# Seven-product up projection: all products of a half unit made wide, the third factor summed by an adding transfer, and another order of the seven

## The chip, the cores and the metric

One core of one Trainium2 chip runs the whole kernel. The metric is the device time of one execution in microseconds (us), given as the median of several runs. The profile beside it is one execution taken by the hardware profiler. A difference of 0.3% is 5.7 us here.

## The reference, cut to what matters

One layer on a sequence of 512 tokens and 2048 channels, in float32: a mixing part (attention and pooling), then a gated feed-forward part. The change touches only the up projection of the second part:

```python
h = rms_norm(x, pre_ffn_g[l])
up = causal_dwconv(h @ w_up[l], conv_w[l], conv_b[l])          # w_up: 2048 x 11264
y = (gelu(up[..., :D_FF], approximate=True) * up[..., D_FF:]) @ w_down[l]
x = x + rms_norm(y, post_ffn_g[l])
```

## The kernel before

**Precision.** Every float32 operand is kept as two parts, a high part rounded to fp32r and the remainder. Making them from a weight block of 128 x 1024 takes two steps of `split`: ACT writes the high part (`wfh`, L143, "rounding" below), DVE subtracts it from the block and writes the low part (`wfl`, L144, "remainder"). A product then needs high x high, high x low and low x high.

**Half units.** The up projection is cut into 44 half units `k` (0 to 43), each of 256 output channels. Half unit `k` is a 2 x 2 block product done with seven block products instead of eight. `i` from 1 to 7 names a product and the weight factor that goes with it; `seven(k, i)` (L941) issues it. Odd half units close a unit: there the gate of the even half is multiplied with the convolved odd half.

**Two forms of a product.** The plain form (L948, `mm3` L159 to L161) has 24 matmuls of 256 columns, three for each of eight weight blocks. The wide form (`wide`, L954 to L962) has eight matmuls of 512 columns, in which the high weights meet the high and the low half of `h` side by side, and eight of 256 columns for the low weights. Its two halves of 256 columns in the bank must be added afterwards. From half unit 5 on (`EARLY = 5`, `PAIRED = 4`) products 3 to 7 are wide; 1 and 2 are plain, and share bank 0, a half each.

**Emptying the banks.** Bank 0: `begin_z` (L880), an ACT copy and one DVE add, after product 2. Bank 1 (product 6): `finish_six` (L892), two DVE adds out of the bank and then two in SBUF. Products 5 and 7: one pair of banks, `keep_pair` (L886). Products 3 and 4: two pairs in turn, by `k % 2`, emptied by two DVE adds of `keep_all` (L1194); then the convolution runs (`taps`: ACT L1155, DVE L1156 and L1157, two of each), in odd half units two DVE products (L1173) and the store of the gate from POOL's queue.

**Weight factors.** A factor is a sum of weight blocks, formed in place: a block is loaded by a DMA from SP's queue (L623), and further blocks are added by DMAs with `accum_op=add` from POOL's queue (L803), each issued once the factor made before from the same buffer has its remainder. Buffer `x` serves factors 4, 5, 6 and 3 in turn, `y` serves 1 and 7, `z` serves 2 and, in half units 5 and later, is added to `x` by DVE (L811) for factor 3.

**Order.** The tensor engine runs in the order of the program; ACT, DVE and POOL run in order too, in an order that a planner fixes when the kernel is built: of the instructions that are ready it takes the one that stands first in the program. `Factors` makes each factor four products ahead, and there are four pairs of `wfh`/`wfl`: the factor of product n+4 goes into the pair that product n leaves. The order of the seven products is written out in `self.order`. In a half unit `k` it is 4, 1, 2, then 6 and 3 of `k - 1`, then 5 and 7. After product 1 of each half unit from 6 on, one of 32 steps that sum `w_down` blocks for the next stage is issued (`wd_sums`), half as copies from SP's queue, half as adding transfers from POOL's.

Of the kernel before, what the change touches and what calls it, by code (L numbers as in the profile page):

```python
# [11 lines left out]
AF = mybir.ActivationFunctionType  # L12
# [18 lines left out]
EARLY = 5  # L31
PAIRED = EARLY - 1
CU = 4
AHEAD = 3
T = S // 2
# [42 lines left out]
def encoder_layer(ctx: ExitStack, tc: tile.TileContext, x, xT, vecs, rel, post_mix, post_ffn,  # L78
# [7 lines left out]
    nc = tc.nc  # L86
# [18 lines left out]
    def bank(name, at=None):  # L105
        if at is None:
            at = cycle.pop(0)
            cycle.append(at)
        pool = psum if at < 2 else upper_pool
        return pool.tile([P, 512], F32, tag=f"ps{at}", bufs=1, name=name)  # L110
# [7 lines left out]
    def w4(name):  # L118
        return big.tile([P, 1024], F32R, tag="w4", bufs=8, name=name)
# [7 lines left out]
    early = const.tile([P, P], F32, name="early")  # L127
# [13 lines left out]
    def split(hi, lo, src, scale=None):  # L141
        if scale is None:
            rounded = nc.scalar.activation(hi, src, AF.Copy)  # L143
            nc.vector.tensor_sub(lo, src, f32(hi))  # L144
        else:
            rounded = nc.scalar.activation(hi, src, AF.Copy, scale=scale)
            nc.vector.scalar_tensor_tensor(lo, src, scale, f32(hi), op0=ALU.mult, op1=ALU.subtract)
        split.last = rounded.ins
        return rounded.ins
# [25 lines left out]
    def part(w, *idx):  # L175
        return tuple(v[(slice(None),) + idx] for v in w)
# [24 lines left out]
    def qk_specs(h):  # L201
        return halves(f"q{h}", w_in, head_cols("q", h), 8, P), halves(f"k{h}", w_in, head_cols("k", h), 8, P)
# [8 lines left out]
    for h in range(1, HEADS):  # L211
        q, k = qk_specs(h)
# [51 lines left out]
    for kb in range(KD):  # L264
        i, o = divmod(kb, 8)
# [9 lines left out]
        for what in "qk":  # L275
            _, hi, lo = first[f"{what}0_{i}"]
# [13 lines left out]
    with tc.tile_pool(name="p1", bufs=2, reuse_waits="tile") as p1:  # L290
# [39 lines left out]
        def project(name, between=None):  # L330
            ps = bank(name)
            next(summing, None)
            for i in range(2):
                if i and between:
                    between()
                w = weights.get(f"{name}_{i}")
                for j in range(8):
                    kb = 8 * i + j
                    mm3(ps, part(w, j), blk(hT, kb), kb == 0, kb == KD - 1)
            return ps  # L340
# [121 lines left out]
        q1 = project("q1", spread1)  # L462
# [142 lines left out]
    def side(name):  # L605
        return ps_.tile([P, S], F32, tag="side", bufs=1, name=name)
# [127 lines left out]
    class Factors:  # L734
# [3 lines left out]
        def __init__(self):  # L738
            n = 2 * NU

            self.order = [(k, i) for k in range(EARLY) for i in (1, 2)]
            self.order += [(0, 5), (0, 7), (1, 5), (0, 6), (1, 7), (1, 6), (0, 3), (1, 3), (0, 4), (1, 4)]
            self.order += [(j, i) for i in (4, 7, 5, 6, 3) for j in (2, 3)]
            for k in range(EARLY - 1, n):
                late = [(k - 1, 6), (k - 1, 3)]
                if k < EARLY:
                    o = [(k, 4), (k, 5), (k + 1, 4), (k, 7)]
                elif k == n - 1:
                    o = [(k, 4), (k, 1), (k, 5), (k, 2), *late, (k, 6), (k, 7)]
                else:  # L750
                    o = [(k, 4), (k, 1), (k, 2), *late, (k, 5), (k, 7)][k == EARLY:]
                self.order += o
            self.order += [(n - 1, 3)]
            self.last = n - 1
            self.alone = *range(EARLY), n - 1
            self.raw, self.made, self.loaded, self.used = {}, [], 0, 0
            self.held = {"x": [], "r": []}
            self.homes = []
# [46 lines left out]
        def make(self, k, i):  # L805
            early, what = k < EARLY, self.source(k, i)
            v = self.raw[k, what]
            if i == 6 and k in (2, 3):
                nc.vector.tensor_add(v, v, self.raw.pop((k, "w")))
            if i == 3 and k:  # L810
                nc.vector.tensor_add(v, v, self.raw.pop((k, "u" if early else "z")))  # L811
            hi, lo = self.homes.pop(0) if self.homes else (w4("wfh"), w4("wfl"))
            split(hi, lo, v)
            if i == 4 and k not in self.alone:
                self.add(k, "x", 1, 0)
            elif i == 1 and not early:
                self.add(k, "y", 1, 0)
            elif i == 5 and k not in (2, 3):
                self.add(k, "x", 0, 0)
            elif i == 6 and not k:  # L820
                self.add(k, "x", 0, 1)
            elif not (i == 6 or i == 2 and not early or i in (4, 7) and k in (2, 3)):
                del self.raw[k, what]
            self.made.append(tuple(v.rearrange("p (a b) -> p a b", a=8) for v in (hi, lo)))

# [25 lines left out]
    def flat(v):  # L851
        return v.rearrange("p a b -> p (a b)")

    p3, factors = None, Factors()
    banks, gates, zs, t57, pairs = {}, {}, {}, {}, None
# [17 lines left out]
    def pair_bank(k, i):  # L873
        tag = "57" if i in (5, 7) else "34"
        if (k, tag) not in banks:
            n = 2 if tag == "57" else k % 2
            banks[k, tag] = pairs.tile([P, 2, S], F32, tag=f"pair{n}", bufs=1, name=f"q{tag}_{k}")
        return banks[k, tag][:, int(i in (7, 4)), :]

    def begin_z(k):  # L880
        z = zs[k] = flat(new_z())
        q12 = banks.pop((k, "12"))[0]
        nc.scalar.activation(z[:, 3 * T:], q12[:, :T], AF.Copy)
        nc.vector.tensor_add(z[:, :T], q12[:, T:], z[:, 3 * T:])  # L884

    def keep_pair(k):  # L886
        q57 = banks.pop((k, "57"))
        t57[k] = v = side("t57").rearrange("p (a b) -> p a b", a=2)
        nc.scalar.activation(v, q57[:, :, :T], AF.Copy)
        nc.vector.tensor_add(v, q57[:, :, T:], v)  # L890
# [47 lines left out]
    def both(f, kb):  # L938
        return f[kb // 4][:, :, kb % 4, :]

    def seven(k, i):  # L941
        w = factors.get()
        if k < PAIRED or i < 3:
            if k > PAIRED and (k, "12") not in banks:
                banks[k, "12"] = bank(f"q12_{k}", 0),
            ps, half = half_bank(k, i)
            for kb in range(8):
                mm3(ps[:, half], part(w, kb), at(h_f[i], kb), kb == 0, kb == 7)  # L948
            return
        if i == 6:  # L950
            ps = banks[k, "6"] = bank(f"q6_{k}", 1)
        else:
            ps = pair_bank(k, i)
        def wide(kb):  # L954
            nc.tensor.matmul(ps.rearrange("p (a b) -> p a b", a=2), w[0][:, kb], both(h_f[i], kb),  # L955
                             start=kb == 0, stop=kb == 7)

        for kb in range(7):
            wide(kb)
        for kb in range(8):  # L960
            nc.tensor.matmul(ps[:, :T], w[1][:, kb], at(h_f[i], kb)[0], start=False, stop=False)  # L961
        wide(7)  # L962
# [11 lines left out]
    with tc.tile_pool(name="p2", bufs=1, reuse_waits="tile") as p2:  # L974
# [112 lines left out]
        for n in (5, 3):  # L1087
            B = new_banks(f"m{n}", 4 if n == 5 else 0)
            for cc in range(2):
                late = (lambda q: h0.append(next(turning))) if n == 3 else None  # L1090
                h0, ps = [], [B[cc, t] for t in range(2)]
# [67 lines left out]
    def new_z():  # L1159
        return p3.tile([P, 2, S], F32, tag="z", name="z")  # L1160
# [75 lines left out]
    for k, i in rest:  # L1236
        if k == PAIRED and pairs is None:
            begin_z(k)
            singles.close()
            pairs = up_banks.enter_context(  # L1240
                tc.tile_pool(name="pairs", bufs=1, space=bass.MemoryType.PSUM, reuse_waits="tile"))
            for n in (1, 2, 0):
                pairs.tile([P, 2, S], F32, tag=f"pair{n}", bufs=1, name="place")
        seven(k, i)
        if k > PAIRED and i == 2:
            begin_z(k)
        done.setdefault(k, set()).add(i)
        if i == 1 and k > EARLY:
            next(summing, None)
        if k >= PAIRED and i in (5, 7) and {5, 7} <= done[k]:  # L1250
            keep_pair(k)
        if (k, i) == (end, 7):
            finish_six(k)
            next_first()
        if (k, i) == (end, 4):
            for n in (1, 2):
                rights[0].send(-n)
        if (k, i) == (end - 1, 3):
            next_first()
        if (k, i) == (2, 6):  # L1260
            continue
        if i == 6:
            if k == 3:
                keep_six(2)
            if k < PAIRED:
                keep_six(k)
            elif k < end:
                finish_six(k)
            if k == 1:
                begin_z(2)  # L1270
        if i == (4 if k < 2 else 3):
            keep_all(k)
            if k == 1:
                begin_z(3)
# [255 lines left out]
```

## Time and profile before

| | before |
|---|---|
| runs | median 1898.94 us of 3 (1895.9 to 1900.63) |
| profiled execution | 1897.62 us, of which the span of the profile is 1895.8 us |
| granted clock of the tensor engine | 0.995 over the span |
| busy share of the span | PE 99%, PEld 86%, DVE 77%, ACT 50%, POOL 16% |

PE is the tensor engine's matmuls, PEld its weight loads, DVE the vector engine, ACT the scalar engine, POOL the engine whose queue also issues adding DMAs. Matmuls overlap, so that the distance between starts, not the duration of one, is what a matmul costs; the same holds in part for DVE and ACT, whose instructions overlap by some hundredths of a us.

### The profile page before, as it was taken

Reading aid. Unit: us, or ns where it says so; the run is one execution under the profiler, and the core shown is the slowest. Engines: PE = TensorE matmul, PEld = TensorE weight load, DVE = VectorE, ACT = ScalarE, POOL = GpSimd, SP = SyncE. Lnnn points to the kernel's source line nnn. Section 1 sums busy time; section 2 is a strip of 40 time slices with the busy share of each in tenths; the row PEclk is TensorE's granted clock in tenths of the full one; section 3 lists DMA queues with packets and bytes.
Section 4 is the critical chain, followed back from the end, with each engine's and each line's share of the span. In section 5 each row is a group of like instructions: output and inputs, shape, how many; then the busy total and the mean of one; then the engine's idle time right before and its main releaser. Section 6 shows DMA issues by size and latency. Waiting matters only on the chain. (4 is left out here: it accounts for less than half of the span.)

```text
span 1895.8 us, 26426 instructions
## 1 busy us (share of the span) xinstructions
PE 1870.9 (99%) x10298; PEld 1631.7 (86%) x10298; DVE 1467.0 (77%) x1743; ACT 952.6 (50%) x1174; POOL 301.4 (16%) x396
## 2 busy tenths in 40 slices
PE   9999999999999999999999999999999999999998
PEld 7888888888889989999999999999997778888886
DVE  5554346587688888888888888888889689998877
ACT  6333233355487554555545555445545555465543
POOL 4100000000011111112221121121110112222221
PEclk9999999999999999999999999999999999999999
DMA  9747847576877877777888778778677889999998
GB/s 328 220 117 177 241 115 195 152 192 220 280 274 203 237 184 191 206 195 190 203 196 218 193 191 220 189 194 201 175 158 258 294 246 243 257 236 239 222 226 239
DMA packets 181949, 403.55 MB, mean 213 GB/s; under 512 B 11584, under 2 KB 63168, under 8 KB 179264
## 3 DMA queue, kind: packets, MB, share of 16 engines
q1 hardware_dynamic: 134480, 257.66, 40.9%
q0 software_dynamic: 47344, 144.20, 39.3%
q8 instruction: 81, 1.33, 0.3%
q14 instruction: 44, 0.36, 0.1%
HBM read 345.19 MB, written 106.95 MB: 238 GB/s over the span
## 5 line engine op out<-in xcount | busy, mean ns | idle before, releaser
L143 ACT ACTIVATE wfh<-wx 128x1024 fp32r<-128x1024 f32 x167 | 173.3, 1059 | 209.4 <-DVE wx L811 134.1
L955 PE MATMUL q<-h,wfh 128*128 128x512 f32 x960 | 254.7, 394 | 2.4 <-DVE z L884 2.4
L144 DVE TENSOR_TENSOR wfl<-wx,wfh 128x1024 fp32r<-128x1024 f32 x167 | 200.8, 1222 | 51.8 <-ACT wfh L143 51.7
L160 PE MATMUL p<-bl,ah 128*128 128x512 f32 x560 | 220.2, 393 | 6.2 <-DVE bl L144 6.2
L161 PE MATMUL p<-bh,al 128*128 128x512 f32 x560 | 219.9, 393 | 1.2 <-DVE al L144 1.2
L159 PE MATMUL p<-bh,ah 128*128 128x512 f32 x560 | 219.7, 392 | 1.3 <-DVE t L890 1.3
L159 PE MATMUL q<-gT,wfh 128*128 128x256 f32 x752 | 213.2, 283 | 1.1 <-DVE z L918 1.1
L160 PE MATMUL q<-gT,wfh 128*128 128x256 f32 x752 | 213.1, 283 | 0.2 <-DVE gT L144 0.2
L161 PE MATMUL q<-gT,wfl 128*128 128x256 f32 x752 | 212.9, 283 | 0.0
L955 PEld LDWEIGHTS q<-h,wfh 128*128 128x128 f32 x960 | 176.0, 189 | 32.3 <-DVE z L884 2.7
L143 ACT ACTIVATE bh<-b 128x2048 fp32r<-128x2048 f32 x70 | 133.6, 1915 | 86.0 <-DVE b L679 64.1
L955 PE MATMUL q<-gT,wfh 128*128 128x512 f32 x640 | 167.2, 392 | 0.4 <-DVE t L890 0.4
L144 DVE TENSOR_TENSOR bl<-b,bh 128x2048 fp32r<-128x2048 f32 x70 | 159.3, 2285 | 9.5 <-PE p L160 5.2
L803 POOL DMA_DIRECT2D wx<-in_w_up x87 | 76.5, 879 | 532.0 <-DVE wfl L144 446.2
L160 PEld LDWEIGHTS q<-gT,wfh 128*128 128x128 f32 x752 | 142.2, 189 | 2.1 <-DVE gT L144 0.4
L159 PEld LDWEIGHTS q<-gT,wfh 128*128 128x128 f32 x752 | 142.4, 189 | 1.3 <-ACT wfh L143 1.3
L161 PEld LDWEIGHTS q<-gT,wfl 128*128 128x128 f32 x752 | 142.2, 189 | 0.0
L961 PEld LDWEIGHTS q<-h,wfl 128*128 128x128 f32 x960 | 131.8, 192 | 9.5
L143 ACT ACTIVATE wfh<-wy 128x1024 fp32r<-128x1024 f32 x82 | 87.1, 1062 | 103.9 <-PE q L961 65.7
L955 PEld LDWEIGHTS q<-gT,wfh 128*128 128x128 f32 x640 | 118.0, 189 | 21.2 <-DVE t L890 0.6
L961 PE MATMUL q<-h,wfl 128*128 128x256 f32 x960 | 134.7, 283 | 0.0
L160 PEld LDWEIGHTS p<-bl,ah 128*128 128x128 f32 x560 | 106.2, 190 | 30.3 <-DVE bl L144 8.3
(441 smaller groups left out, 4130.5 us busy)
## 6 DMA issues: line engine op xcount, KB each, us to landing
wx<-in_w_up POOLq DMA_DIRECT2D x87, 512.0 KB, 8.1
b<-in_w_down SPq DMA_DIRECT2D x38, 1024.0 KB, 9.8
sum<-part POOLq DMA_DIRECT2D x70, 512.0 KB, 8.7
wx<-in_w_up SPq DMA_DIRECT2D x45, 512.0 KB, 3.6
wy<-in_w_up SPq DMA_DIRECT2D x44, 512.0 KB, 4.5
wz<-in_w_up SPq DMA_DIRECT2D x44, 512.0 KB, 5.9
wy<-in_w_up POOLq DMA_DIRECT2D x39, 512.0 KB, 8.4
wo_sum<-in_w_o POOLq DMA_DIRECT2D x16, 1024.0 KB, 11.8
```

The costliest lines, as they stand in the source:

```text
L143: rounded = nc.scalar.activation(hi, src, AF.Copy)
L144: nc.vector.tensor_sub(lo, src, f32(hi))
L159: nc.tensor.matmul(ps, l[0], r[0], start=first, stop=False)
L160: nc.tensor.matmul(ps, l[0], r[1], start=False, stop=False)
L161: nc.tensor.matmul(ps, l[1], r[0], start=False, stop=last)
L803: self.last_add = nc.gpsimd.dma_start(self.raw[k, what], self.block(k, m, kh), accum_op=ALU.add).ins
L955: nc.tensor.matmul(ps.rearrange("p (a b) -> p a b", a=2), w[0][:, kb], both(h_f[i], kb), start=kb == 0, stop=kb == 7)
L961: nc.tensor.matmul(ps[:, :T], w[1][:, kb], at(h_f[i], kb)[0], start=False, stop=False)
```

## The change

Products 1 and 2 of the half units from 5 on are issued in the wide form as well, product 1 into bank 0 and product 2 into bank 1, which product 6 uses too. `begin_z` is replaced there by `begin_one` after product 1 (ACT copy, DVE add) and `begin_two` after product 2 (two DVE adds). For the half units 5 to 42 the DVE add for factor 3 is replaced by an adding DMA from POOL's queue, issued after factor 6 has its remainder. The order becomes 4, 6 of `k - 1`, 1, 2, 5, 3 of `k - 1`, 7; the last half unit has an order of its own.

```diff
                 if k < EARLY:
                     o = [(k, 4), (k, 5), (k + 1, 4), (k, 7)]
+                elif k == EARLY:
+                    o = [(k, 1), (k, 2), late[0], (k, 5), late[1], (k, 7)]
                 elif k == n - 1:
-                    o = [(k, 4), (k, 1), (k, 5), (k, 2), *late, (k, 6), (k, 7)]
+                    o = [(k, 4), late[0], (k, 5), (k, 1), (k, 2), late[1], (k, 6), (k, 7)]
                 else:
-                    o = [(k, 4), (k, 1), (k, 2), *late, (k, 5), (k, 7)][k == EARLY:]
+                    o = [(k, 4), late[0], (k, 1), (k, 2), (k, 5), late[1], (k, 7)]
...
-            if i == 3 and k:
+            if i == 3 and (0 < k < EARLY or k == self.last):
                 nc.vector.tensor_add(v, v, self.raw.pop((k, "u" if early else "z")))
...
-            elif i == 6 and not k:
+            elif i == 6 and not (0 < k < EARLY or k == self.last):
                 self.add(k, "x", 0, 1)
-            elif not (i == 6 or i == 2 and not early or i in (4, 7) and k in (2, 3)):
+            elif not (i == 6 or i == 2 and k == self.last or i in (4, 7) and k in (2, 3)):
                 del self.raw[k, what]
...
+    def begin_one(k):
+        z, q1 = flat(new_z()), banks.pop((k, "1"))
+        zs[k] = z
+        nc.scalar.activation(z[:, 3 * T:], q1[:, :T], AF.Copy)
+        nc.vector.tensor_add(z[:, 3 * T:], q1[:, T:], z[:, 3 * T:])
+
+    def begin_two(k):
+        z, q2 = zs[k], banks.pop((k, "2"))
+        nc.vector.tensor_add(z[:, :T], q2[:, :T], z[:, 3 * T:])
+        nc.vector.tensor_add(z[:, :T], q2[:, T:], z[:, :T])
...
-        if k < PAIRED or i < 3:
-            if k > PAIRED and (k, "12") not in banks:
-                banks[k, "12"] = bank(f"q12_{k}", 0),
+        if k < PAIRED or k == PAIRED and i < 3:
...
-        if i == 6:
-            ps = banks[k, "6"] = bank(f"q6_{k}", 1)
+        if i in (1, 2, 6):
+            ps = banks[k, str(i)] = bank(f"q{i}_{k}", int(i != 1))
...
         seven(k, i)
+        if k > PAIRED and i == 1:
+            begin_one(k)
         if k > PAIRED and i == 2:
-            begin_z(k)
+            begin_two(k)
```

## Rows read from the trace of the kernel before

**Rows 1.** The page, part 1: busy us, share, instructions of each engine.

```profile
PE 1870.9 (99%) x10298; PEld 1631.7 (86%) x10298; DVE 1467.0 (77%) x1743; ACT 952.6 (50%) x1174; POOL 301.4 (16%) x396
```

**Rows 2.** Windows: length, busy us of PE, PEld, DVE, ACT, POOL, clock, DMA share, GB/s.

```profile
900.00:919.72 19.72, 19.72 (x130) 18.03 (x128) 17.36 (x22) 9.47 (x12) 4.53 (x6) 1.00 0.81 186
919.72:939.45 19.73, 19.73 (x129) 18.05 (x128) 16.17 (x20) 10.55 (x13) 3.98 (x5) 1.00 0.89 216
680.00:1425.00 745.00, 745.00 (x4826) 680.98 (x4825) 631.13 (x792) 379.52 (x436) 141.18 (x167) 1.00 0.79 195
...
1600.00:1700.00 100.00, 100.00 (x443) 82.77 (x442) 96.80 (x66) 55.97 (x50) 23.84 (x20) 1.00 1.02 243
```

**Rows 3.** Timeline of PE: start us, duration us, engine, line, [idle before, releaser].

```profile
667.11 1.20 PE L955 MATMUL q<-h,wfh 128*128 128x512 f32 x4 [2.42 <-DVE z L884]
...
904.39 1.12 PE L961 MATMUL q<-gT,wfl 128*128 128x256 f32 x8
...
909.97 1.11 PE L961 MATMUL q<-h,wfl 128*128 128x256 f32 x8
...
911.16 0.28 PE L159 MATMUL q<-gT,wfh 128*128 128x256 f32 x1
...
916.92 1.78 PE L955 MATMUL q<-h,wfh 128*128 128x512 f32 x7
...
919.72 0.62 PE L955 MATMUL q<-gT,wfh 128*128 128x512 f32 x2
```

**Rows 4.** Timeline of DVE, columns as before.

```profile
666.64 0.42 DVE L884 TENSOR_TENSOR z<-q,z 128x256 f32<-128x256 f32 x1
...
900.18 0.88 DVE L896 TENSOR_TENSOR z<-q,z 128x256 f32<-128x256 f32 x2 [0.27 <-PE q L955]
901.05 1.22 DVE L144 TENSOR_TENSOR wfl<-wx,wfh 128x1024 fp32r<-128x1024 f32 x1
...
907.78 1.41 DVE L1156 SCALAR_TENSOR_TENSOR cb<-z,vec,cb 128x511 f32<-128x511 f32 x2
...
911.63 1.22 DVE L144 TENSOR_TENSOR wfl<-wx,wfh 128x1024 fp32r<-128x1024 f32 x1
912.76 0.68 DVE L890 TENSOR_TENSOR t<-q,t 128x512 f32<-128x512 f32 x1
913.36 1.22 DVE L811 TENSOR_TENSOR wx<-wx,wz 128x1024 f32<-128x1024 f32 x1
...
919.92 0.89 DVE L896 TENSOR_TENSOR z<-q,z 128x256 f32<-128x256 f32 x2 [0.22 <-PE q L955]
```

**Rows 5.** Groups of instructions, 700 to 1400: count | busy, mean ns | idle before.

```profile
L1194 DVE TENSOR_TENSOR z<-q,z 128x512 f32<-128x512 f32 x72 | 49.5, 688 | 4.1 <-DVE z L899 0.5
L811 DVE TENSOR_TENSOR wx<-wx,wz 128x1024 f32<-128x1024 f32 x35 | 42.6, 1216 | 0.0
...
L884 DVE TENSOR_TENSOR z<-q,z 128x256 f32<-128x256 f32 x36 | 15.0, 417 | 0.0
```

**Rows 6.** Timeline of ACT.

```profile
919.68 1.06 ACT L143 ACTIVATE wfh<-wx 128x1024 fp32r<-128x1024 f32 x1 [1.31 <-PE q L961]
```

**Rows 7.** Timeline of POOL.

```profile
902.57 0.89 POOL L803 DMA_DIRECT2D wx<-in_w_up  x1 [3.36 <-DVE wfl L144]
...
1422.31 0.85 POOL L803 DMA_DIRECT2D wx<-in_w_up  x1 [2.84 <-DVE wfl L144]
```

**Rows 8.** Timeline of SP's queue.

```profile
1423.70 1.27 SPq L623 DMA_DIRECT2D b<-in_w_down  x2
```

**Rows 9.** Waits of SP's queue, 676 to 1420: total us, times, longest.

```profile
SPq L623 <- DVE wfl L144: 697.1, 38, 25.5
```

**Rows 10.** DMA view, 900 to 1000: queue, packets, MB, share of 16 engines.

```profile
q0 software_dynamic: 3360, 12.06, 58.2%
```

**Rows 11.** DMA view, 1422.2 to 1423.6: issues, KB each, us to landing.

```profile
wx<-in_w_up POOLq DMA_DIRECT2D x1, 512.0 KB, 5.5
```

**Rows 12.** Line L803, 700 to 1400: all adding transfers of weight blocks.

```profile
DMA to landing us min/median/max: 5.2/8.4/12.1
```

## The prediction

> **What bounds the kernel now.** First the page's busy shares: PE is busy 99% of the span, DVE 77% [rows 1]. A share over the whole span says little about one stage, so next the windows: from 680 to 1425 us, where the half units from 5 on run, PE is busy 745.00 of 745.00 at full clock, DVE 631 (85%), and the DMA engines 79% [rows 2]. PE waits for nothing there. So this stage lasts as long as PE's stream; anything taken from another engine gains nothing, and anything that makes PE wait is a loss. Then the two neighbouring half units: one takes 19.73 us; DVE is busy 17.36 in the one with the odd tail (the two gate products, L1173), 16.17 in the other [rows 2]. DVE has slack on average, but little in the odd tail. That is where I look.
>
> **What the wide form is worth.** Distances between starts count. The low-weight matmuls of wide products two apart start at 904.39 and 909.97: 5.58, 2.79 us a product. Two plain products run from 911.16 to 916.92: 5.76, 2.88 each [rows 3]. (Check: 5 x 2.79 + 2 x 2.88 = 19.7.) So a product gains 0.088 us. Half units 5 to 43 are 39, with two products each: 78 x 0.088 = 6.8 us. This is the largest gain that PE's stream can give. A half unit would take 7 x 2.79 = 19.55.
>
> The Trainium skill, "TensorE: Matmul & The Clock Gate", section "Back-to-back issue gap", gives a warm distance of N/2.4 + 2.5 ns: by it a plain product is 24 x 109.2 = 2.62 us and a wide one 8 x 215.8 + 8 x 109.2 = 2.60, a gain of 0.02 and of 1.6 us over all 78 (an estimate from that page). The rows show longer distances and a larger gain, and the sum goes by the rows.
>
> **DVE.** Removed: 38 adds L811, 1216 ns each. Added: two adds of 256 columns per half unit, 417 ns each as L884 [rows 5]. Net 1.22 - 0.83 = 0.38 us less per half unit, so DVE's total is no problem: by itself 0 on the path, as PE covers it.
>
> **The gaps that the new order leaves.** Two banks are now needed again after a single product. Bank 1: product 6, product 1, then product 2 into the bank that 6 used. And the pair of 3 and 4: product 3 of k-1, product 7, then product 4 of k+1 into the same pair; before, two products lay between. If DVE has not emptied the bank within 2.79 us, PE stands. After an add PE starts 0.05 later (L884 ends at 667.06, PE starts at 667.11) [rows 3, 4]; DVE can read a bank 0.20 after the next product's start (919.72 and 919.92) [rows 3, 4].
>
> For product 3 that is easy: its two adds come 0.20 after its end and last 2 x 0.69 [rows 5], 1.58 of 2.79. For product 6 I lay out DVE's queue in the odd case by the planner's rule, from the end of product 3 of an odd k-1 (t = 0). Durations are distances between starts:
> - 0.20 until the bank can be read, the two adds of product 3: 1.38, a remainder 1.13 (911.63 to 912.76) [rows 4]: t = 2.71.
> - Four convolution steps and two gate products: 907.78 to 911.63, 3.85 [rows 4]: t = 6.56.
> - Remainder 1.13, the add of `keep_pair` 0.60 (912.76 to 913.36) [rows 4], remainder 1.13: t = 9.42.
> - The two adds of product 6: 0.88 [rows 4]: t = 10.30.
>
> Product 2 wants bank 1 after products 7, 4, 6 and 1: t = 4 x 2.79 = 11.17. That fits by 0.8. But the remainder of factor 3 also becomes ready near 9.42: it takes the pair that product 6 itself leaves at t = 8.37, and ACT's rounding, which starts as soon as PE leaves the pair, lasts 1.06 [rows 6], so it is ready at 9.47. If it goes in front of the second add or of both, the adds end at 11.43, PE starts at 11.48, 0.3 late. It stands first in the program and the tie is within 0.05; I take 0.3 us in each of the 19 odd cases, with bounds 0 (both adds go first) and 1.4 (one more remainder of 1.13 gets in front): +5.7 us, 0 to 27. In the even case the 1.2 us of gate products are missing and the adds come in time: 0.
>
> **Half unit 5.** Its order is 1, 2, then 6 of half unit 4: products 2 and 6 follow each other into bank 1. PE must wait 0.20 + 0.88 + 0.05 = 1.1 us, once; 2.4 if a remainder is in front. I take 1.1.
>
> **The adding transfers.** 38 more on POOL's queue, 0.9 us of POOL each [rows 7]. Behind one that waits for factor 6's remainder stand only the `wd_sums` step and the stores of the gate; nothing on PE's path waits for these. All sums in a buffer now have four products between two factors where they had five: 11.17 us. A sum is issued some 3.4 us after its pair opens (rounding 1.06, remainder 1.22, 0.3 to POOL's start [rows 4, 7], and about 0.8 behind other work of ACT: an estimate), and if it lands more than 8.4 us later, the next remainder comes late, pushing the adds that empty product 3 into the odd tail, which has no slack. Landings now: 5.2 / 8.4 / 12.1 us at minimum, median, maximum [rows 12]. That median is of sums issued behind three loads. SP's loads wait for a DVE remainder [rows 9], that of factor 3; it now comes one product after factor 5's, so the loads start 1 to 2 us behind the sum of factor 5 instead of in front of it. The row nearest to this: a sum issued at 1422.31 with loads from 1423.70 on landed after 5.5 us [rows 7, 8, 11]. So I take 0, with late landings as a rival.
>
> The Trainium skill, "DMA: Bandwidth & Descriptors", section "Queues, rings and completion order", says that each DMA engine takes turns between its queues packet by packet. By that the sum would share with the loads from their start: at most its own 2.5 us more, a landing at 8.0 and still no wait.
>
> DMA work: 12.06 MB took 58.2% of 100 us [rows 10], so 0.52 MB take 2.5 us of all engines. A half unit has 0.81 to 0.89 of 19.73 us [rows 2], 16.0 to 17.6; with 2.5 more 18.5 to 20.1 of 19.55. That is at the edge where a step of `wd_sums` runs too. At a share of 1.02, 1600 to 1700, PE still ran 100.00 of 100.00 [rows 2], so a full DMA alone costs nothing here.
>
> ACT keeps its single copy. The last half unit's order leaves two products between 6 and 2, one between 2 and 6: no wait by the same sums. At the end of the stage PE may gain or lose a few us; I put 0, within 2.
>
> **Sum.** -6.8 + 5.7 + 1.1 = 0.0: the profiled time stays at 1897.6. That execution lies 1.3 below the median of the runs, so in their terms 1899. A change below 0.3%, 5.7 us, can't be told from none.
>
> **Rivals.**
> - No wait in the odd tail: both adds of product 6 go ahead of the remainder. -6.8 + 1.1 = -5.7: 1893, just at the edge of "faster". For it: the adds are ready at 8.57, the remainder only at 9.47. Against: DVE gets to them at 9.42, so it hangs on hundredths. 0.22.
> - Slower, the transfers: the sum for factor 6 lands late. It decides from 8.4 us on; each us beyond goes into at least the 19 odd tails and at most all 38 half units. At 9.3: 0.9 x 19 to 38 = 17 to 34, about 1925. For it: the median is 8.4 already and the engines get 14% more work. Against: the landing of 5.5 with loads behind it. 0.20.
> - Slower, DVE: a further remainder gets in front of product 6's adds. 19 x 1.4 = 27, so -6.8 + 27 + 1.1 = +21: 1920. For it: DVE runs without a break for 9 us there. Against: the planner saw the same tie and the next pair opens only at 11.17. 0.13.
> - The wide form does not bring 0.088 in bank 0 and 1 (by a gain of 0.02 a product): -1.6 + 5.7 + 1.1 = +5: 1904. Against: products 3 to 7 are the same instructions. 0.05.
>
> **Chances.** Forecast 0.40, its own range 1895 to 1903. Faster by over 0.3%: half of the first rival and a little for the stage's end, 0.13. Within 0.3%: forecast, the other half, half of the last, 0.54. Slower: 0.33. The range leaves out the lower half of the first rival and the upper half of the transfers': 1892 to 1925.
>
> **What would show it.** In the new profile L955 and L961 starts 2.79 apart in all products; plain L159 to L161 matmuls of 256 columns 39 x 16 fewer each. A half unit of 19.55 us with an even k-1, about 19.85 with an odd one. PE's waits: L955 for DVE's adds of `finish_six`, about 0.3 us, some 19 times, and one of 1.1 to 2.4 for `begin_two`, near 665 to 680. No L811 after half unit 5 except in the last. ACT's wait for L811 (gone) must not come back as a wait for the DMA of `wx`. I am wrong if PE waits for `keep_all`'s adds, if landings of `wx` on POOL's queue have a median over 8.4, or if waits come in the even half units too.

## The result, and the profile after

The changed kernel takes 1913.86 us in the median of four runs (1911.01 to 1917.56), the one before 1897.43 in four runs beside it: a ratio of 1.0086, 95% interval [1.0069, 1.0102]. It is slower by 16.4 us. The profiled execution of the changed kernel took 1917.56 us (span 1915.8), the slowest of its four; that of before 1897.62 (span 1895.8). What follows is made against these two spans, 20.0 us apart.

The page, part 1, answers to [rows 1]:

```profile
PE 1872.4 (98%) x9674; PEld 1601.4 (84%) x9674; DVE 1457.7 (76%) x1783; ACT 954.7 (50%) x1174; POOL 334.1 (17%) x434
```

PE has 624 matmuls fewer, which is 39 x 16, and DVE 9 us less work. Both are what the change was to do, and yet the span grew. The windows show where: columns as in [rows 2]; the first is a half unit with an odd tail, the second its neighbour, the third the whole stage.

```profile
747.87:767.98 20.11, 19.79 (x114) 17.18 (x112) 17.08 (x23) 9.60 (x12) 4.97 (x7) 1.00 0.94 238
767.98:787.53 19.55, 19.55 (x113) 17.21 (x112) 15.89 (x21) 10.55 (x13) 3.42 (x5) 1.00 0.90 216
680.00:1425.00 745.00, 730.19 (x4147) 638.34 (x4148) 609.30 (x815) 372.42 (x426) 169.35 (x200) 1.00 0.93 217
```

The even half unit is the 19.55 us forecast. The odd one takes 20.11, 0.56 more. Over the stage PE stands for 14.8 of 745 us where it stood for none, and the DMA engines went from 79% to 93%. The waits of PE from 680 to 1425 name the place (waited for, total us, times, longest); L967 is the wide product's first matmul (L955 before), L909 the adds of `finish_six` (L896 before), L1206 those of `keep_all`:

```profile
PE q L967 <- DVE z L909: 13.7, 18, 3.3
PE q L967 <- ACT wfh L143: 1.1, 1, 1.1
PE q L967 <- DVE z L1206: 0.9, 1, 0.9
```

Eighteen waits, one in each odd tail of the window, all for the two adds that empty product 6. Eleven of them look alike. One of them on PE, against [rows 3]:

```profile
757.86 1.12 PE L973 MATMUL q<-gT,wfl 128*128 128x256 f32 x8
758.81 0.39 PE L967 MATMUL q<-gT,wfh 128*128 128x512 f32 x1
759.52 1.86 PE L967 MATMUL q<-gT,wfh 128*128 128x512 f32 x7 [0.32 <-DVE z L909]
761.22 0.98 PE L973 MATMUL q<-gT,wfl 128*128 128x256 f32 x7
```

and on DVE, against [rows 4]:

```profile
755.52 0.69 DVE L903 TENSOR_TENSOR t<-q,t 128x512 f32<-128x512 f32 x1
756.12 2.46 DVE L144 TENSOR_TENSOR wfl<-wx,wfh 128x1024 fp32r<-128x1024 f32 x2
758.50 0.88 DVE L909 TENSOR_TENSOR z<-q,z 128x256 f32<-128x256 f32 x2
```

Behind the add of `keep_pair` stand two remainders, the second of them that of factor 3, and only then the two adds of product 6. They end at 759.38, PE starts at 759.52. The row says 0.32 us idle, but the low-weight matmuls of the two products start 761.22 - 757.86 = 3.36 apart instead of 2.79: 0.57 is lost. The idle time is counted from a modelled end of the last matmul, so the distance of starts is the price.

The other seven waits are longer. The longest, on PE and on DVE:

```profile
1320.19 0.39 PE L967 MATMUL q<-gT,wfh 128*128 128x512 f32 x1
1323.87 2.14 PE L967 MATMUL q<-gT,wfh 128*128 128x512 f32 x7 [3.29 <-DVE z L909]
1325.82 1.91 PE L973 MATMUL q<-gT,wfl 128*128 128x256 f32 x8
```

```profile
1321.71 1.23 DVE L144 TENSOR_TENSOR wfl<-wx,wfh 128x1024 fp32r<-128x1024 f32 x1 [2.64 <-ACT wfh L143]
1322.85 0.88 DVE L909 TENSOR_TENSOR z<-q,z 128x256 f32<-128x256 f32 x2
```

The same remainder of factor 3 is in front, and it is itself late: ACT's rounding started at 1320.62, as the added transfer of factor 3, issued at 1309.04, took 11.5 us to land. ACT's row, and the DMA view from 1309 to 1309.5:

```profile
1320.62 1.06 ACT L143 ACTIVATE wfh<-wx 128x1024 fp32r<-128x1024 f32 x1 [2.81 <-PE q L967]
```

```profile
wx<-in_w_up POOLq DMA_DIRECT2D x1, 512.0 KB, 11.5
```

ACT's row names PE as what released it, because a product happened to end at 1320.58; but product 6 had left the pair near 1317.8, and in all seven long cases the rounding starts 0.1 us after the landing, here at 1320.52. In these seven the transfer landed 8.5 to 11.5 us after its issue, in the eleven others 6.1 to 8.1. The landings as a whole did not get later; all adding transfers, 700 to 1400, against [rows 12]:

```profile
DMA to landing us min/median/max: 5.3/7.2/11.5
```

q0's share from 900 to 1000, against [rows 10]:

```profile
q0 software_dynamic: 4059, 14.61, 75.6%
```

At the end of the stage, waits of PE from 1425 to 1470, and ACT there:

```profile
PE q L967 <- DVE t L903: 3.0, 1, 3.0
PE q L967 <- DVE z L897: 1.3, 1, 1.3
```

```profile
1436.36 1.06 ACT L143 ACTIVATE wfh<-wx 128x1024 fp32r<-128x1024 f32 x1 [5.37 <-DMA wx<-in_w_up]
```

ACT stands 5.4 us for the sum of a factor of the last half unit, and with it, in ACT's order, the convolution and the copy of `keep_pair`, for whose bank PE then waits.

The sum over the stage, in distances of starts beyond 2.79: 18 odd tails x 0.57 = 10.3; 8.0 more in the seven late ones; 1.3 behind the longest of them, where the granted clock had fallen; 1.2 for `keep_all`, once; at the stage's end 6.4, where the kernel before lost 0.7; 1.4 more at its start, of which 1.3 is the wait at half unit 5. Less 6.8 for the wide form that is 21.1; the first and the last wide product of the stage lie 20.7 further apart than before, and the rest is rounding of the distances.

### The profile page after: what moved, and what is told of

The parts are those of the page before. It is cut to its first block, busy times and chain, and to the rows that moved or that the text cites. A ratio compares the mean times of both kernels' runs of the same rounds, so it can differ in the third digit from the quotient of the medians.

```text
span 1915.8 us, 25312 instructions
## 1 busy us (share of the span) xinstructions
PE 1872.4 (98%) x9674; PEld 1601.4 (84%) x9674; DVE 1457.7 (76%) x1783; ACT 954.7 (50%) x1174; POOL 334.1 (17%) x434
## 4 chain that ended last, share of the span: by engine, by line
PE 75%; DVE 8%; DMA 7%; issue 6%; ACT 2%; POOL 1%; SPq 0%; POOLq 0%; DVEq 0%; ACTq 0%
PE q L967 17%; PE q L973 9%; PE p L161 6%; PE p L160 6%; PE p L159 6%; DMA wx<-in_w_up 5%; DVE wfl L144 2%; PE q L159 2%; PE q L160 2%; PE q L161 2%; PE m L160 2%; PE m L161 2%; PE m L159 2%; PE u L159 2%; PE v L159 2%
## 5 line engine op out<-in xcount | busy, mean ns | idle before, releaser
L967 PE MATMUL q<-gT,wfh 128*128 128x512 f32 x1264 | 329.7, 395 | 16.7 <-DVE z L909 13.7
L967 PEld LDWEIGHTS q<-gT,wfh 128*128 128x128 f32 x1264 | 231.2, 190 | 62.3 <-issue 18.9
L967 PE MATMUL q<-h,wfh 128*128 128x512 f32 x960 | 248.9, 394 | 5.8 <-DVE z L886 2.6
L967 PEld LDWEIGHTS q<-h,wfh 128*128 128x128 f32 x960 | 176.1, 190 | 37.9 <-DVE z L886 2.9
L805 POOL DMA_DIRECT2D wx<-in_w_up x125 | 109.0, 872 | 561.8 <-DVE wfl L144 454.7
L973 PEld LDWEIGHTS q<-gT,wfl 128*128 128x128 f32 x1264 | 173.8, 192 | 12.7
L973 PE MATMUL q<-gT,wfl 128*128 128x256 f32 x1264 | 177.4, 283 | 0.0
L161 PEld LDWEIGHTS p<-bh,al 128*128 128x128 f32 x560 | 106.7, 191 | 24.4 <-DVE al L144 2.3
L159 PEld LDWEIGHTS p<-bh,ah 128*128 128x128 f32 x560 | 106.4, 190 | 23.2 <-DVE t L903 0.6
L718 POOL DMA_DIRECT2D sum<-part x60 | 71.9, 1222 | 257.6 <-DVE part L709 111.5
L144 DVE TENSOR_TENSOR wfl<-wy,wfh 128x1024 fp32r<-128x1024 f32 x82 | 100.0, 1220 | 13.1 <-ACT wfh L143 13.0
```

The lines of the kernel that those rows point to most:

```text
L159: nc.tensor.matmul(ps, l[0], r[0], start=first, stop=False)
L161: nc.tensor.matmul(ps, l[1], r[0], start=False, stop=last)
L718: nc.gpsimd.dma_start(dest, v, accum_op=ALU.add)
L805: self.last_add = nc.gpsimd.dma_start(self.raw[k, what], self.block(k, m, kh), accum_op=ALU.add).ins
```

## The experiments

Theory "gap": product 2 waits for bank 1 because product 6's adds stand behind the remainder of factor 3, and one product in between is too little; a late sum acts only through that remainder. Rival "transfers": 38 more adding transfers on nearly full DMA engines hold PE up wherever they end. Rival "DVE": the 0.83 us of adds that each half unit got are the cost. Each kernel was timed beside the kernel before on the same chip, in three groups, in which the kernel before had medians of 1897.2, 1897.3 and 1897.8 us.

| kernel | median, us | ratio to before, 95% |
|---|---|---|
| wide products, old order, DVE add | 1891.69 | 0.9967 [0.9955, 0.998] |
| plain products, new order, transfer | 1899.78 | 1.0014 [1.0003, 1.0025] |
| wide, new order, DVE add | 1944.14 | 1.0247 [1.0231, 1.0263] |
| wide, new order, transfer: the change | 1913.86 | 1.0086 [1.0069, 1.0102] |
| the same, adds of 6 first in the program | 1907.64 | 1.0061 [1.0038, 1.0084] |
| the same, without `wd_sums` | 1905.42 | 1.0043 [1.0031, 1.0056] |
| the same, two products between 6 and 2 | 1896.41 | 0.9993 [0.9985, 1.0002] |
| that, another last half unit | 1897.71 | 1.0004 [0.9995, 1.0013] |
| that, last product 6 in bank 0 | 1895.18 | 0.9983 [0.9974, 0.9992] |
| first row, last half unit 5 before 6 and 3 | 1896.91 | 1.0002 [0.9993, 1.001] |
| first row, last half unit 5 after 6 and 3 | 1897.26 | 1.0 [0.9991, 1.0009] |

**Product 6's adds first in the program.**

```diff
-        w = factors.get()
+        w = factors.get(3 if PAIRED <= k < end and i == 6 else 4)
...
                 finish_six(k)
+                factors.prefetch(4)
```

> The kernel after, but in the program the two adds that empty product 6 stand ahead of the making of factor 3, so that DVE takes them first; transfers, products, order of the seven and amount of work are those of after. Theory 'gap' (product 2 waits for bank 1 because product 6's adds stand behind factor 3's remainder; late sums act only through that remainder): the waits for `finish_six`, 11 x 0.57 + 12.0 = 18.3 us of product distances in the profile of after, go, and the time is 1913.9 - 18 = 1896, between 1893 and 1901. Rival 'transfers' (38 more adding transfers on nearly full DMA engines, whose late sums hold the tensor engine wherever they end): the waits move to another product, 1908 to 1916. Rival 'DVE' (the 0.83 us of added adds in each half unit are the cost): nothing changes, 1910 to 1916.

Measured 1907.64 (1904.26 to 1919.09): 6 us gained instead of 18, a miss. The profile is of the slowest of its six executions, 1919.09. DVE's timeline in an odd tail tells why:

```profile
798.50 1.22 DVE L144 TENSOR_TENSOR wfl<-wx,wfh 128x1024 fp32r<-128x1024 f32 x1
799.63 0.42 DVE L909 TENSOR_TENSOR z<-q,z 128x256 f32<-128x256 f32 x1
799.96 1.22 DVE L144 TENSOR_TENSOR wfl<-wx,wfh 128x1024 fp32r<-128x1024 f32 x1
801.09 0.42 DVE L909 TENSOR_TENSOR z<-q,z 128x256 f32<-128x256 f32 x1
```

The second add needs the result of the first, and the remainder of factor 3 was put between the two. In this profile the short loss fell from 0.57 to 0.32 a tail, and a late sum still stands in front: seven tails with one cost 12.3 us, where the seven of the changed kernel cost 12.0. The edit did not do what its expectation supposed; it leaves the theories open.

**Without `wd_sums`.**

```diff
-            in_turn(b, w_block(1, 1, c, cs) if i == 3 else wd_sum[i][:, :, cs])
+            in_turn(b, w_block(1, 1, c, cs))
...
-        if i == 1 and k > EARLY:
-            next(summing, None)
```

> The kernel after without the 32 steps that sum blocks of w_down during this stage (left out of the computation: the next stage loads plain blocks of the same size in place of those sums). This takes DMA work out of the stage and leaves the order of DVE's instructions. Theory 'gap': the short waits of 0.57 us in each odd half unit stay, since they hang on DVE's order alone, 19 x 0.57 = 11; the long ones, where the sum of factor 5 or 3 landed late, shrink to the same 0.57: 1913.9 - 12 + 7 x 0.57 = 1906, between 1904 and 1910. Rival 'transfers': with the engines relieved all waits go, 1895 to 1900. Rival 'DVE': 1910 to 1916.

Measured 1905.42. The adding transfers land sooner, and every odd tail from 700 to 1400 loses 0.55 to 0.58 us, with no long wait left. Landings of the adding transfers, then the waits of PE from 680 to 1425:

```profile
DMA to landing us min/median/max: 5.2/5.6/7.9
```

```profile
PE q L967 <- DVE z L909: 5.8, 18, 0.3
```

So the short loss is DVE's order alone, and the long ones are the late sum on top: as "gap" has it, and not "transfers".

**The wide form alone.** The order and the DVE add of before; products 1 and 6 in bank 0, 2 in bank 1.

```diff
-        if k < PAIRED or i < 3:
+        if k < PAIRED or k == PAIRED and i < 3:
...
-        if i == 6:
-            ps = banks[k, "6"] = bank(f"q6_{k}", 1)
+        if i in (1, 2, 6):
+            ps = banks[k, str(i)] = bank(f"q{i}_{k}", int(i == 2))
```

> One part of the change alone: products 1 and 2 wide, with the order of before and the DVE add for factor 3 of before. Bank 0 holds 1 and then 6, bank 1 holds 2, so that 6 is followed by four products before its bank is wanted, and one product stands between 1 and 6. Theories 'gap' and 'transfers' both say that the wide form's 78 x 0.088 = 6.8 us come out nearly whole: 1890 to 1894. Rival 'DVE': 1.22 us of the factor's add stay and 0.83 us of new adds come on top, in each half unit; the odd tail of DVE, which has no slack, gets later and the tensor engine waits there: 1905 or more.

Measured 1891.69, 5.5 us faster than before and the fastest kernel of the study. DVE is busier than before [rows 2], and PE stands for 2 us only; the window from 680 to 1425:

```profile
680.00:1425.00 745.00, 743.03 (x4255) 653.42 (x4254) 659.30 (x872) 381.58 (x437) 140.89 (x168) 1.00 0.80 197
```

659 us of DVE against 609 in the changed kernel: "DVE" as a matter of amount falls. The adding transfers here, 38 fewer, land later than in the changed kernel (median 8.4 us, up to 12.1), so a late landing by itself is no price either.

**The order and the transfer alone.** Products 1 and 2 plain in bank 0, bank 1 for product 6.

```diff
-        if k < PAIRED or k == PAIRED and i < 3:
+        if k < PAIRED or i < 3:
+            if k > PAIRED and (k, "12") not in banks:
+                banks[k, "12"] = bank(f"q12_{k}", 0),
...
-        if k > PAIRED and i == 1:
-            begin_one(k)
         if k > PAIRED and i == 2:
-            begin_two(k)
+            begin_z(k)
```

> The kernel after with products 1 and 2 plain again, sharing bank 0 as before; the new order and the adding transfer for factor 3 stay, and bank 1 is product 6's alone. Theory 'gap': nothing wants bank 1 soon after product 6, so no wait for `finish_six`; the gain of the wide form (6.8) is gone, and what remains is the start and the end of the stage, some 6 to 8 us in the profile of after: 1897.4 + 5 to 8 = 1902 to 1906. Rival 'transfers': the late sums cost what they cost in after, and the wide form's gain is missing: 1915 to 1921. Rival 'DVE' (adds of 0.83 us a half unit are the cost): 1895 to 1899.

Measured 1899.78, 2.6 above before; "gap" had said 1902 to 1906 and was too high by 2 to 6, as it reckoned too much for the start and the end of the stage. The adding transfers are as many and land as late (median 7.3 us, up to 11.1), the DMA engines are as full (0.93), and from 680 to 1425 PE waits once:

```profile
PE q L969 <- DVE z L1208: 1.2, 1, 1.2
```

Late sums cost nothing where no bank is wanted soon. "Transfers" falls here.

**Two products between 6 and 2.**

```diff
-                    o = [(k, 4), late[0], (k, 1), (k, 2), (k, 5), late[1], (k, 7)]
+                    o = [(k, 4), late[0], (k, 1), (k, 5), (k, 2), late[1], (k, 7)]
```

> The kernel after with products 2 and 5 exchanged in every half unit from 6 on but the last: 4, 6 of the half unit before, 1, 5, 2, 3 of the half unit before, 7. The same instructions, transfers and bytes; what changes is that two products (1 and 5) stand between 6 and 2 in bank 1 instead of one, 5.58 us instead of 2.79. Theory 'gap': product 6's adds are late by at most the 0.57 us (and 3.8 where a sum lands late), so that 2.79 us more cover nearly all; the waits for `finish_six` go, 18.3 us, and the fall of the clock behind the longest of them: 1913.9 - 18 to 20 = 1894 to 1896, up to 1900 if a late sum still reaches through. Rival 'transfers': the sums are as many and as late, and hold the tensor engine at another place: 1905 to 1914.

Measured 1896.41, 17.5 below the changed kernel. The same instructions, the same bytes; from 700 to 1418 all products start 2.79 apart. ACT still waits for sums, more than the 32.2 us (16 times) of the changed kernel; the waits of ACT from 680 to 1425, then of PE:

```profile
ACT wfh L143 <- DMA wx<-in_w_up: 58.1, 35, 3.4
```

```profile
PE q L967 <- DVE z L897: 2.0, 1, 2.0
PE q L967 <- DVE t L903: 0.8, 1, 0.8
```

No wait for `finish_six` is left; the two that stand there lie at the window's edges, in half units 5 and 43. An odd tail on DVE and on PE shows why:

```profile
756.74 1.23 DVE L144 TENSOR_TENSOR wfl<-wx,wfh 128x1024 fp32r<-128x1024 f32 x1
757.88 0.88 DVE L909 TENSOR_TENSOR z<-q,z 128x256 f32<-128x256 f32 x2
```

```profile
754.44 1.12 PE L973 MATMUL q<-h,wfl 128*128 128x256 f32 x8
760.98 2.00 PE L967 MATMUL q<-gT,wfh 128*128 128x512 f32 x8
```

Factor 3's remainder is in front again, and the two adds end at 758.76, which is 4.3 us behind the start of product 6's low-weight matmuls (754.44). That is as late as in the eleven short cases of the changed kernel (759.38 against 755.07), and so it is in 14 of the 18 odd tails; in the other four a late sum makes it up to 5.6. The changed kernel wants the bank after 3.97 us, this one, for the second matmul of the row at 760.98, after 6.76. This settles it: the distance of 6 and 2 is the cause, and DVE's order and the late sum are what fills it. It is no cover without an end: the longest case of the changed kernel, 7.3 us, would have reached through here too.

**The DVE add in the new order.**

```diff
-            if i == 3 and (0 < k < EARLY or k == self.last):
+            if i == 3 and k:
...
-            elif i == 6 and not (0 < k < EARLY or k == self.last):
+            elif i == 6 and not k:
```

> The kernel after with the DVE add for factor 3 of before in place of the adding transfer; wide products and the new order stay. 38 adds of 1.22 us come back to DVE, 38 adding transfers of 0.52 MB go. Theory 'gap', with late landings only as what lengthens it: the waits behind late sums go, the short ones of 0.57 us in each odd half unit stay: 1913.9 - 12 + 7 x 0.57 = 1906 if DVE covers its added work, and up to 19 x 1.22 = 23 more if the odd tail does not: 1904 to 1929. Rival 'transfers': with the engines relieved nothing of the loss is left: 1895 to 1900.

Measured 1944.14, above the range of "gap". The waits for `finish_six` stayed, and another one came, for the other bank that the new order wants after a single product, the pair of 3 and 4. The waits of PE over the whole span, then DVE:

```profile
PE q L967 <- DVE z L1206: 18.8, 38, 3.6
PE q L967 <- DVE z L909: 15.9, 18, 0.9
```

```profile
915.63 1.23 DVE L813 TENSOR_TENSOR wx<-wx,wz 128x1024 f32<-128x1024 f32 x1
916.77 0.68 DVE L1206 TENSOR_TENSOR z<-q,z 128x512 f32<-128x512 f32 x1
917.37 1.22 DVE L144 TENSOR_TENSOR wfl<-wy,wfh 128x1024 fp32r<-128x1024 f32 x1
918.50 0.68 DVE L1206 TENSOR_TENSOR z<-q,z 128x512 f32<-128x512 f32 x1
```

The add stands in front of `keep_all`'s adds, and a remainder between them, in all 38 half units. So the adding transfer is worth 30 us in the new order; the order is what needs it.

**The end of the stage.** Four kernels change the last half unit alone. Two on the kernel with two products between 6 and 2: product 1 before 5 in the last half unit, and product 6 of half unit 43 in bank 0.

```diff
-                    o = [(k, 4), late[0], (k, 5), (k, 1), (k, 2), late[1], (k, 6), (k, 7)]
+                    o = [(k, 4), late[0], (k, 1), (k, 5), (k, 2), late[1], (k, 6), (k, 7)]
```

> The kernel of the run before (two products between 6 and 2), and in the last half unit too product 1 goes ahead of 5, so that three products lie between 7 of half unit 42 and 5 of half unit 43, which take the same pair of banks, instead of two. In the profile of after the wait there was 3.03 us, and the product behind it ran 1.3 us longer at a lower granted clock. If this price is the order's, 3 to 4.4 us less than the run before: 1890 to 1893 by theory 'gap', 1901 to 1911 by 'transfers'; if it is the stage's end, whatever the order, no difference from the run before.

```diff
-            ps = banks[k, str(i)] = bank(f"q{i}_{k}", int(i != 1))
+            ps = banks[k, str(i)] = bank(f"q{i}_{k}", int(i == 2 or i == 6 and k < factors.last))
```

> The kernel with products 2 and 5 exchanged, and in the last half unit product 6 put into bank 0, which product 1 left three products before, instead of bank 1, which product 2 left one product before. The wait there was 3.08 us of the profile, 4.08 with the lower clock behind it. If the bank's distance is the price: 1896.4 - 4 = 1892.4. Rival: DVE's add that empties bank 0 stands behind the same late remainder of factor 7 (ACT waits for its sum), and ends only 1.0 us before the adds that empty bank 1: 1895 to 1896.

Measured 1897.71 and 1895.18. The first gained nothing: the wait for `keep_pair` went, and one of 5.4 us for the add of product 2 came. The second lies 1.2 lower, where its rival had it, but the two intervals overlap, so that this gain is not shown. Two on the wide products in the old order:

```diff
-                    o = [(k, 4), (k, 1), (k, 5), (k, 2), *late, (k, 6), (k, 7)]
+                    o = [(k, 4), (k, 1), (k, 2), (k, 5), *late, (k, 6), (k, 7)]
```

> The wide products in the order of before, with another order for the last half unit: 4, 1, 2, 5, 6 and 3 of the half unit before, 6, 7, so that three products stand between 7 of half unit 42 and 5 of half unit 43 where two stood. In the profile of the wide products in the old order 2.19 us were lost there. Expected: 1891.7 - 2.2 = 1889.5, between 1888 and 1892; 1891 to 1893 if the wait moves to the next product.

```diff
-                    o = [(k, 4), (k, 1), (k, 5), (k, 2), *late, (k, 6), (k, 7)]
+                    o = [(k, 4), (k, 1), (k, 2), *late, (k, 5), (k, 6), (k, 7)]
```

> The wide products in the order of before, with the last half unit in the same order as the others as far as possible: 4, 1, 2, 6 and 3 of the half unit before, 5, 6, 7. Four products stand between 7 of half unit 42 and 5 of half unit 43, where two stood and 2.19 us were lost; 6 follows 5. If the price is that distance: 1891.7 - 2 = 1889.5, between 1888 and 1891. If the end of the stage is bound by DVE and by the sums that the last factors wait for, the wait moves as it did with the other order tried (7.1 us at product 6): 1892 to 1897.

Measured 1896.91 and 1897.26, both 5 us slower than the order they were to mend. In the first PE stands 6.4 us for the adds of `finish_six`, in a stretch where ACT stood 8.5 for a sum; in the second, where 6 follows 5 at once, 2.9 us for ACT itself, which stood 10.4. ACT and PE in the second:

```profile
1433.48 1.06 ACT L143 ACTIVATE wfh<-wx 128x1024 fp32r<-128x1024 f32 x1 [10.44 <-DMA wx<-in_w_up]
```

```profile
1434.59 2.69 PE L964 MATMUL q<-h,wfh 128*128 128x512 f32 x7 [2.89 <-ACT wfh L143]
```

The order of the last half unit sets how long each sum may take, and none of the four was shown to be better at it. Which is best for the changed kernel stays open.

## Why the prediction was right and wrong

The forecast was no change, 1899 us with 1895 to 1903 as its own range, and the kernel became 16.4 slower. It saw where PE would wait and why; what failed is the size of what it put against the wide form's gain, the adding transfers above all. That 1913.9 still lies between its outer bounds, 1892 and 1925, is owed to the width of these, which take in the lower half of the rival on late transfers, and not to the sum.

- **The wide form: right.** 0.088 us a product, 6.8 in all; alone it gave 5.5, in the profile with 2.2 lost at the last half unit. The formula of the Trainium skill, "TensorE: Matmul & The Clock Gate", section "Back-to-back issue gap", which the page gives for a single, isolated matmul, makes the gain 1.6 us (the estimate ahead of the result); the runs stand with the rows, not with it.
- **The even half unit and the place of the wait: right.** 19.55 us; the odd tail, `finish_six`, factor 3's remainder ahead of both adds, 18 times in the window. PE also waited for `keep_all`, which the prediction had put at nothing and named as a sign of being wrong: once, 1.2 us. **Half unit 5: right,** 1.3 us once where 1.1 was taken (680.20, where PE's next product starts 0.16 behind the second add of `begin_two`; the profile names ACT there, which ended 0.05 later than that add).
- **The size of the short wait: too small.** The term 5.7 (0.3 x 19) measured 0.57 x 18 = 10.3. PE started 0.48 late instead of 0.3 (759.52 against 756.25 + 2.79 = 759.04): the adds ended 0.34 late where 0.26 was reckoned, and from their end to PE's start it took 0.14 where 0.05 was taken. And PE's first matmuls behind a wait lost another 0.10 (759.52 to 761.22 is 1.70, where 756.25 to 757.86 is 1.61).
- **The adding transfers: the term that failed by most.** Taken as 0, by a landing of 5.5 with loads behind it. Measured 8.0, and 1.3 by the lower clock. The rival "Slower, the transfers" named the late landing and its point, 8.4 us, but put it at 17 to 34 us, in at least all 19 odd tails. It was the sum of factor 3, not 6, it passed that point in 7 of 18 tails, and it did not act by way of product 3's adds, as reckoned, but by factor 3's own remainder in front of product 6's adds. What is over the short loss goes roughly with landing minus 8.4: at 9.4 us 0.89, at 10.0 us 1.47, at 11.5 us 3.22; at 8.1 us nothing. (The one of 8.5 us lost 0.65, as it was also issued 0.66 later than the others.) One row from the quick end of [rows 12] had been taken for all. What the prediction had as a sign, a median of landings over 8.4, was no sign: the median fell to 7.2, and the tails were late. From the rule of the Trainium skill, "DMA: Bandwidth & Descriptors", section "Queues, rings and completion order", an estimate of 8.0 was worked out for a sum that shares with the loads; the seven landed later than that by 0.5 to 3.5, so by it too there would have been no wait.
- **The stage's end: too small.** 0, within 2, was taken, 5.7 was measured (6.4 against 0.7). That two products lie between banks said nothing of ACT, which waits there for a sum in front of the copy of `keep_pair`.
- **DVE's total, ACT, a second remainder in front: right at nothing.**
- **What the parts say.** The wide form alone is -5.5, the order with the transfer alone +2.6, both +16.4. The 19 us between lie in bank 1, which only the two together want back after one product: the distance that the prediction had named, and priced at 5.7.

## What to carry to other kernels

Before a bank or buffer is shared, count the work that lies between its last use and its next against the longest queue in front of the instruction that empties it, late arrivals included; a cover that fitted by 0.8 us on paper was none here, and exchanging two entries of the order bought it for nothing. Try the parts of a change apart: here one half of it alone beats both kernels. Where a sum is made by a transfer, take the slow end of its landings at the DMA share that the new stage will have, not a quick row.

## What the runs showed of the hardware

Behind the longest wait, of 3.29 us, PE's granted clock was at its lower level, 1.2 GHz, for some 3 us. Windows of the changed kernel around the wait of 3.29 us (the clock is the third figure from the end):

```profile
1322.00:1325.00 3.00, 1.13 (x5) 0.99 (x6) 2.93 (x5) 1.33 (x2) 0.00 (x0) 1.00 1.10 214
1325.00:1328.00 3.00, 3.00 (x14) 2.67 (x13) 1.26 (x3) 0.24 (x1) 0.00 (x0) 0.54 0.95 198
1328.00:1332.00 4.00, 4.00 (x22) 3.43 (x21) 1.98 (x3) 1.79 (x2) 0.89 (x1) 0.92 0.91 311
```

Eight low-weight matmuls took 1.91 us at 1325.82, where they take 1.12; the next product started 1.3 late. So this wait cost its length and 1.3 us. Behind the waits of 0.3 to 1.3 us between 900 and 1000 the granted clock stayed at 1.00. The length of a wait does not decide it alone: in the kernel with two products between 6 and 2, PE waited 3.05 us up to 666.64, as long as at the stage's end of the changed kernel (3.03, clock 0.50 behind it), and there the granted clock stayed at 1.00. What decides between the two was not measured.

The executions of one kernel lie apart by different amounts: the wide products in the old order by 1.6 us in five runs, the changed kernel by 6.5 in four, and the one with product 6's adds first by 14.8 in six. What varies from run to run was not measured.
